# Another engine for one bank copy, and an earlier turn of four feature blocks, in a squared-ReLU MLP on one Trainium2 core

## Chip, core and metric

One Trainium2 chip, one of its cores. The metric is device microseconds of one execution of the whole program; the time of a kernel is the median of its runs. TensorE multiplies out of SBUF into PSUM; ScalarE and VectorE move results out of PSUM and prepare weights; DMAs load the weights.

## The reference

A decoder trunk of two layers on 256 tokens of width 2048, in float32. Each layer has a mixer (recurrent in layer 0, attention in layer 1), a residual add, and an MLP; the change concerns the MLP alone:

```python
def squared_relu_mlp(h, w1, w2):
    return jnp.square(jax.nn.relu(h @ w1)) @ w2
...
        h = h + mix
        h = h + squared_relu_mlp(rms_norm(h, norm_mlp[layer]), mlp_w1[layer], mlp_w2[layer])
```

`w1` is 2048 x 8192 and `w2` 8192 x 2048. Everything must come out with float32 precision.

## The kernel before

**Precision.** Every weight tile `raw` (128 x 2048) is split into `hi`, rounded by ScalarE (L102), and `lo = raw - hi` by VectorE (L103), and each operand likewise; a product is then three matmuls, hi·hi, hi·lo and lo·hi (`times`, 12 matmuls of 512 columns for four feature blocks). Weight tiles are fetched two units ahead, in the order of the list `units`, with three buffers each for `raw`, `hi` and `lo`.

**The MLP.** Each layer's MLP runs over four quarters of 2048 hidden features. In a quarter, `first` makes two pairs (n0 = 0, then n0 = 2) of hidden blocks of 512 with `w1`, and `second` two pairs of output blocks with `w2`. Both go through `blocks`. Half of a pair's work, on feature blocks 0 to 7, is done by seven products in Strassen's manner (`a`, `t1`, `t2`, `c`, `t3`, `d`, `t4`) on sums and differences of weights (`s`, `t`) and of operands (`formx`, `formh`); the other half, on blocks 8 to 15, by plain products (`n2`, `n3` for the one hidden block of the pair, `n6`, `n7` for the other), each for both halves of the tokens. The order for the first matrix is a, t1, n6, t2, c, n7, t3, d, n2, t4, n3. Products are collected in four PSUM banks, alpha, beta, gamma, delta: a and t2 go to beta, t1 and c to alpha. Some products are needed twice. Then an event behind the product copies the bank as it stands into an SBUF tile (`hold`: y1 after a, y4 after t1, y2 after t2), and the bank is added to further. n6 is 12 matmuls into delta and then 12 into alpha, so the alpha half has to wait until t1's content has been copied to y4. In the second matrix the event behind such a product is a VectorE operation that adds the bank into the residual (`to_x`, L751).

**Feature blocks.** The MLP reads its operand with features on partitions. The output projection before it (`out_project`) ends with tokens on partitions; `to_features(n)` turns four feature blocks of it with eight transposes on TensorE, and ScalarE (L235) and VectorE (L236) scale and split them into `bufa`. It is not run at once but put on the list `later`; `flush` runs what is on the list. `tokens` flushes after each weight tile, and `blocks` after each plain product what was on the list when that product began. So `to_features(3)`, blocks 12 to 15, put there at the end of `out_project`, is run behind n6 of the layer's first pair; n7 is the product that reads these blocks. The hidden blocks are turned in the same way for the second matrix (`to_h`), where the tiles of the first pair of hidden blocks (y4 and y2 among them) serve as scratch for the sums in `formh` (L593, L594) while the second pair runs.

**Order.** TensorE's order is the program's: `mm` and `turn` chain every matmul and transpose to the one before. The order on the other engines is set by the tile framework's planner when the kernel is built: at the time it reckons for each point it takes, of the instructions that are ready on an engine, the one with the highest priority. Weight work has its place in the program moved ahead by 150 (`stream`), results of banks and features by 400 (`urgent`). On the chip each engine then runs its list in that order.

Of the kernel before, what the change touches and what calls it, by code (L numbers as in the profile page):

```python
# [41 lines left out]
def trunk_kernel(ctx, tc, x, xtok, cols, tab, masks, pos, fin, w_in, w_gate, w_out, w_qkv, w_o, w1, w2, out):  # L42
# [14 lines left out]
    V, A, T = nc.vector, nc.scalar, nc.tensor  # L57
# [4 lines left out]
    bufa = act.tile([P, KB, 2 * S], F32R, name="bufa")  # L62
# [14 lines left out]
    for step in ORDER.split():  # L77
        src, first, n = where[step[0]]
        units.extend((src, first(int(step[1])) + i) for i in range(n))
# [90 lines left out]
    def unit(src, i):  # L170
        u = at[1]
        assert units[u][0] is src and units[u][1] in (None, i), (u, i)
        at[1] += 1
        if u + 2 >= at[0]:
            fetch()
        return made.pop(u)
# [3 lines left out]
    def mm(*args, **kw):  # L180
        chain[:] = [after(T.matmul(*args, **kw), chain)]  # L181
# [6 lines left out]
    def flush(due=None):  # L188
        todo = later[:due]
        del later[:due]  # L190
        for f in todo:
            f()
# [11 lines left out]
    def lut(out_, in_, func, **kw):  # L204
        i = A.activation(out_, in_, func, **kw)
        if luts["kind"] != tables[func]:
            luts.update(kind=tables[func], before=luts["now"], now=[])
        luts["now"].append(after(i, luts["now"][:1] or luts["before"]))
# [436 lines left out]

    nrm = out_project(w_out, "nmlp0", (2, 3, 0, 1))

    def blocks(src, i0, n0, mov, forms, events, final):
        plain = lambda j, k: (mov[:, k, j * P:j * P + P], mov[:, k, S + j * P:S + j * P + P])
        form = lambda f, k: (forms[:, k, 0, f * P:f * P + P], forms[:, k, 1, f * P:f * P + P])  # L650
        side = {"a": lambda i: plain(0, 2 * i), "d": lambda i: plain(0, 2 * i + 1), "t4": lambda i: plain(1, 2 * i + 1),
                "t1": lambda i: form(3, i), "t2": lambda i: form(0, i), "t3": lambda i: form(1, i),
                "c": lambda i: form(2, i)}
        alpha, delta, gamma = (pmm.tile([P, 512], F32, name="p") for _ in range(3))
        beta = psc.tile([P, 512], F32, name="po" if n0 else "pd", bufs=1)
        bank = {"a": beta, "t1": alpha, "t2": beta, "c": alpha, "t3": beta, "d": gamma, "t4": beta}
        sums = {(0, 0): gamma, (0, 1): beta, (1, 0): alpha, (1, 1): delta}
        opened = []

        def times(bank, w, get):  # L660
            for i in range(4):
                h, l = w.part(i * 512, 512)
                xh, xl = get(i)
                mm(bank, xh, h, start=not any(b is bank for b in opened), stop=False, skip_group_check=True)
                opened.append(bank)
                mm(bank, xh, l, start=False, stop=False, skip_group_check=True)
                mm(bank, xl, h, start=False, stop=i == 3, skip_group_check=True)

        plains = [0, 0]
        for what, u in ORDERS[src is w2]:  # L670
            w = unit(src, None if u is None else i0 + 4 * n0 + u)
            if what != "n":
                times(bank[what], w, side[what])
                if what in events:
                    events[what](bank[what])
                continue
            n, g = divmod(u, 4)
            plains[n] += 1
            due = len(later)
            for j in (1, 0) if n else (0, 1):  # L680
                times(sums[n, j], w, lambda i, j=j, g=g: plain(j, 4 * g + i))
                if plains[n] == 2:
                    final(n, j, sums[n, j])
            flush(due)

    def to_h(n, tiles):
        def work():
            ps = []
            for y in tiles:
                ps.append(psc.tile([P, 4, P], F32, name="pl", bufs=2))  # L690
                for i in range(4):
                    turn(ps[-1][:, i], y[:, i * P:i * P + P])
            with urgent():
                for j, p in enumerate(ps):
                    h = bufb[:, 4 * n:4 * n + 4, j * P:j * P + P]
                    A.copy(h, p)
                    V.tensor_tensor(bufb[:, 4 * n:4 * n + 4, S + j * P:S + j * P + P], p, h.bitcast(F32), OP.subtract)
                if n < 2:
                    z = tiles[1].rearrange("p (k c) -> p k c", k=4)
                    A.copy(z, ps[1])  # L700
                    t = tiles[0].rearrange("p (k c) -> p k c", k=4)
                    (s2, s4), (a21, a22), (a11, a12) = (
                        [v.rearrange("p (m two) c -> p two m c", two=2)[:, e] for e in range(2)] for v in (t, z, ps[0]))
                    combos(a22, s2, a21, s4, a11, a21, a12, a22)
                    for v, at in ((z, slice(1, 4, 2)), (t, slice(0, 4, 2))):
                        part_forms(formh, 2 * n, 2, at, v.rearrange("p (m two) c -> p m two c", two=2))
        later.append(work)

    def first(i0, n0):
        keep, tiles = {}, {}  # L710

        def hold(name, bufs=1):
            def event(bank):
                with urgent():
                    keep[name] = pair.tile([P, 512], F32, name=name, bufs=bufs)
                    A.copy(keep[name], bank)  # L716
            return event

        def relu2(n, j, y, src):
            A.activation(y, src, AF.Relu)  # L720
            A.activation(y, y, AF.Square)  # L721
            tiles[n, j] = y
            if (n, 1 - j) in tiles:
                to_h(n0 + n, (tiles[n, 0], tiles[n, 1]))

        def u3(bank):
            with urgent():
                y = keep["y4"]
                V.tensor_tensor(y, y, bank, OP.subtract)
                V.tensor_tensor(y, keep["delta"], y, OP.add)  # L730
                relu2(1, 1, y, y)

        def final(n, j, bank):
            with urgent():
                if (n, j) == (1, 1):
                    keep["delta"] = bank
                elif (n, j) == (0, 1):
                    y = pair.tile([P, 512], F32, name="y21")
                    relu2(0, 1, y, bank)
                else:  # L740
                    y = keep["y2" if n else "y1"]
                    V.tensor_tensor(y, bank, y, OP.subtract if n else OP.add)
                    relu2(n, j, y, y)

        blocks(w1, i0, n0, bufa, formx, {"a": hold("y1", 2), "t1": hold("y4"), "t2": hold("y2"), "t3": u3}, final)

    def second(i0, n0, nrm, r2, r2n, done, gains):
        def to_x(bank, j, n, r, last):
# [21 lines left out]
    def mlp(layer, nrm, nxt, gname):  # L770
        fing = []

        def gains():
            for n, name in enumerate(("y1", "y1", "y2", "y4")):
                fing.append(pair.tile([P, 512], F32, name=name, bufs=2 if n < 2 else 1))
                nc.gpsimd.dma_start(fing[n], bass.AP(tensor=fin.tensor, offset=fin.offset + 512 * n,
                                                     ap=[[0, P], [1, 512]]))

        r2 = nrm.inv_mean()
        r2n = tmp.tile([P, 2], F32, name="r2n", bufs=2)  # L780
        V.tensor_scalar(r2n, r2, -1.0, None, op0=OP.mult)
        if not gname:
            lut(spare, epsc, AF.Sqrt)
        for q in range(4):
            ends = nxt if q == 3 else None

            def done(n):
                if ends is None:
                    return
                if gname:  # L790
                    to_features(n, gname)
                elif n != LAST:
                    at = slice(n * 512, n * 512 + 512)
                    with urgent():
                        for j in range(2):
                            V.tensor_tensor(xres[:, j, at], xres[:, j, at], fing[n], OP.mult)

            for n in (0, 2):
                first(layer * 64 + q * 16, n)
            for n in (0, 2):  # L800
                second(layer * 64 + q * 16, n, ends, r2, r2n, done, gains if ends and not gname and not n else None)
        return fing

    nx1 = Norm()
    mlp(0, nrm, nx1, "nmix1")
    pairs.close()

# [259 lines left out]
```

## Time and profile before

| | |
|---|---|
| three runs | 2179.17, 2179.26, 2180.12 us, median 2179.26 |
| profiled execution | 2178.8 us; span of the profile 2177.0 us |
| busy in the span | TensorE 99%, VectorE 82%, ScalarE 58%, GpSimd 2% |
| granted TensorE clock | 0.999 |
| HBM read | 460.78 MB, 213 GB/s over the span |
| MLP of layer 0, of layer 1 | from about 426 to 1106 us, from about 1490 us to the end |
| second pair of `first`, layer 0: alpha half of n6 starts at | 479.52, 647.92, 816.32, 984.72 us (168.4 apart) |

PE is TensorE, DVE VectorE, ACT ScalarE, POOL GpSimd, SP SyncE. `p`, `pd` and `po` are PSUM banks: alpha, gamma and delta are `p`, beta is `pd` or `po`. The tiles of `hold` are all called `y` in the trace. A row of the timeline gives start, duration, engine, line, operation, output <- inputs, shapes, how many in a row, and in brackets the idle time before it with what ended it; starts of one row to the next are what tells TensorE's pace, since the ends of matmuls are modelled.

### The profile page before, as it was taken

How to read it: one execution, taken by the hardware profiler on the slowest of the kernel's cores; microseconds unless marked ns; L12 is line 12 of the kernel's file. 1: busy time of each engine (PE TensorE's matmuls, PEld its weight loads, DVE VectorE, ACT ScalarE, POOL GpSimd, SP SyncE). 2: the span in 40 equal slices, each digit the busy share in tenths (PEclk: the TensorE clock that was granted, in tenths of full speed). 3: DMA queues.
4: the chain of work that ended last, by engine and by line, in shares of the span. 5: the costliest groups of instructions: out<-in, count | busy, mean ns of one | idle time of the engine just before them, and what ended most of it. 6: DMA issues, size and time to landing. Idle time of an engine off the chain costs nothing.

```text
span 2177.0 us, 27718 instructions
## 1 busy us (share of the span) xinstructions
PE 2148.7 (99%) x11044; PEld 1834.7 (84%) x11044; DVE 1783.6 (82%) x2078; ACT 1261.1 (58%) x1429; POOL 44.6 (2%) x57
## 2 busy tenths in 40 slices
PE   9999999999999999999999999999999999999997
PEld 8999998878888888888788888888888888888886
DVE  7776787779879889888877778667898898898897
ACT  7444485566466566466554544455655755755664
POOL 0000000000000000000000000000000000000000
PEclk9999999999999999999999999999999999999999
DMA  8444445577777677787655554556768777777873
GB/s 317 155 157 170 149 156 207 189 235 240 228 236 248 226 247 232 232 251 231 201 207 169 179 175 163 185 193 213 232 221 258 237 224 238 251 231 224 260 238 129
DMA packets 65857, 464.68 MB, mean 213 GB/s; under 512 B 7344, under 2 KB 8112, under 8 KB 10304
## 3 DMA queue, kind: packets, MB, share of 16 engines
q1 hardware_dynamic: 58176, 410.89, 53.2%
q0 software_dynamic: 7264, 51.42, 12.8%
q8 instruction: 87, 1.43, 0.3%
q10 hardware_dynamic: 288, 0.61, 0.1%
q14 instruction: 42, 0.34, 0.0%
HBM read 460.78 MB, written 2.10 MB: 213 GB/s over the span
## 4 chain that ended last, share of the span: by engine, by line
PE 89%; ACT 5%; DVE 3%; issue 2%; DMA 1%; SPq 0%; DVEq 0%; ACTq 0%
PE p L181 63%; PE po L181 11%; PE pd L181 10%; ACT hi L102 3%; PE pl L184 2%; DVE lo L103 1%; PE pl L476 1%; DMA raw<-in_w 0%; ACT y L720 0%; ACT formh L593 0%; ACT y L716 0%; ACT y L721 0%; PE pl L864 0%; DMA xall<-in_x 0%; PE po L885 0%
## 5 line engine op out<-in xcount | busy, mean ns | idle before, releaser
L102 ACT CAST hi<-raw 128x1024 fp32r<-128x1024 f32 (+2 forms) x486 | 689.2, 1443 | 571.4 <-PE p L181 403.1
L103 DVE TENSOR_TENSOR lo<-raw,hi 128x1024 fp32r<-128x1024 f32 (+2 forms) x486 | 822.3, 1709 | 237.7 <-ACT hi L102 219.3
L181 PE MATMUL p<-hi,bufb 128*128 128x512 f32 x1408 | 448.5, 390 | 2.2 <-DVE xall L751 2.1
L181 PE MATMUL p<-hi,bufa 128*128 128x512 f32 x1280 | 412.5, 392 | 11.3 <-ACT y L716 7.9
L181 PE MATMUL p<-bufa,hi 128*128 128x256 f32 (+1 forms) x1792 | 364.9, 317 | 0.1
L181 PEld LDWEIGHTS p<-hi,bufb 128*128 128x128 f32 x1408 | 264.3, 188 | 60.0 <-DVE xall L751 5.6
L181 PEld LDWEIGHTS p<-bufa,hi 128*128 128x128 f32 x1792 | 294.5, 190 | 18.9 <-DVE hz L418 0.3
L181 PEld LDWEIGHTS p<-hi,bufa 128*128 128x128 f32 x1280 | 240.4, 188 | 65.5 <-ACT y L716 11.3
L181 PE MATMUL p<-lo,bufb 128*128 128x512 f32 x704 | 274.1, 389 | 1.0 <-DVE lo L103 1.0
L181 PE MATMUL p<-bufa,lo 128*128 128x256 f32 x1152 | 255.5, 287 | 0.0
L181 PE MATMUL p<-lo,bufa 128*128 128x512 f32 x640 | 250.5, 391 | 1.9 <-DVE lo L103 1.9
L103 DVE TENSOR_TENSOR lo<-s,hi 128x2048 fp32r<-128x2048 f32 x96 | 219.5, 2287 | 23.2 <-ACT hi L102 21.3
L102 ACT CAST hi<-s 128x2048 fp32r<-128x2048 f32 x96 | 183.7, 1913 | 48.1 <-PE po L181 21.7
L181 PEld LDWEIGHTS p<-bufa,lo 128*128 128x128 f32 x1152 | 189.3, 191 | 2.7
L181 PEld LDWEIGHTS p<-lo,bufb 128*128 128x128 f32 x704 | 132.2, 188 | 28.3 <-DVE lo L103 1.4
L181 PEld LDWEIGHTS p<-lo,bufa 128*128 128x128 f32 x640 | 120.4, 188 | 27.1 <-DVE lo L103 3.2
L130 DVE TENSOR_TENSOR s<-s,raw 128x2048 f32<-128x2048 f32 x48 | 109.6, 2284 | 1.7 <-DMA raw<-in_w 1.7
L181 PE MATMUL pd<-hi,bufa 128*128 128x512 f32 x256 | 84.8, 392 | 0.0
L181 PE MATMUL po<-hi,bufa 128*128 128x512 f32 x256 | 84.8, 392 | 0.0
L181 PE MATMUL p<-hi,formx 128*128 128x512 f32 x256 | 84.0, 389 | 0.0
L181 PE MATMUL p<-hi,formh 128*128 128x512 f32 x256 | 84.0, 389 | 0.0
L103 DVE TENSOR_TENSOR lo<-t,hi 128x2048 fp32r<-128x2048 f32 x32 | 73.2, 2287 | 12.4 <-ACT hi L102 12.4
(281 smaller groups left out, 2765.7 us busy)
## 6 DMA issues: line engine op xcount, KB each, us to landing
raw<-in_w SPq DMA_DIRECT2D x224, 1024.0 KB, 5.1
raw<-in_w_qkv SPq DMA_DIRECT2D x48, 1024.0 KB, 4.9
raw<-in_w_in SPq DMA_DIRECT2D x46, 1024.0 KB, 4.9
t<-in_w SPq DMA_DIRECT2D x32, 1024.0 KB, 5.4
t<-in_w POOLq DMA_DIRECT2D x32, 1024.0 KB, 8.8
raw<-in_w_out SPq DMA_DIRECT2D x16, 1024.0 KB, 4.9
s<-in_w POOLq DMA_DIRECT2D x16, 1024.0 KB, 8.9
raw<-in_w_o SPq DMA_DIRECT2D x16, 1024.0 KB, 4.9
```

Of the source, the lines that this page charges most:

```text
L102: A.copy(h, w)
L103: V.tensor_tensor(l, w, h.bitcast(F32), OP.subtract)
L130: V.tensor_tensor(held[to], held[x], held[y], OP.add)
L181: chain[:] = [after(T.matmul(*args, **kw), chain)]
L184: chain[:] = [after(T.transpose(out_, in_, ident), chain)]
L476: T.matmul(pl[:, j], kq[:, js], halves(qp[:, js], c, True), start=True, stop=True)
```

## The change

In `first`, y4 is copied out of alpha by VectorE (`V.tensor_copy`) where ScalarE did it (`A.copy`); y1 and y2 stay with ScalarE. And in the first pair of each layer's MLP (quarter 0, n0 = 0) `blocks` flushes the list `later` right behind t1, so `to_features(3)` is run between t1 and n6 where it was run between n6 and t2.

```diff
-    def blocks(src, i0, n0, mov, forms, events, final):
+    def blocks(src, i0, n0, mov, forms, events, final, soon=False):
...
                 if what in events:
                     events[what](bank[what])
+                if what == "t1" and soon:
+                    flush()
                 continue
...
-    def first(i0, n0):
+    def first(i0, n0, soon):
...
-        def hold(name, bufs=1):
+        def hold(name, copy, bufs=1):
             def event(bank):
                 with urgent():
                     keep[name] = pair.tile([P, 512], F32, name=name, bufs=bufs)
-                    A.copy(keep[name], bank)
+                    copy(keep[name], bank)
             return event
...
-        blocks(w1, i0, n0, bufa, formx, {"a": hold("y1", 2), "t1": hold("y4"), "t2": hold("y2"), "t3": u3}, final)
+        blocks(w1, i0, n0, bufa, formx, {"a": hold("y1", A.copy, 2), "t1": hold("y4", V.tensor_copy), "t2": hold("y2", A.copy),
+                                             "t3": u3}, final, soon)
...
-                first(layer * 64 + q * 16, n)
+                first(layer * 64 + q * 16, n, q + n == 0)
```

## The prediction

> **What bounds the kernel now.** I read the page first, for who is busy all the time.
>
> ```profile
> span 2177.0 us, 27718 instructions
> ## 1 busy us (share of the span) xinstructions
> PE 2148.7 (99%) x11044; PEld 1834.7 (84%) x11044; DVE 1783.6 (82%) x2078; ACT 1261.1 (58%) x1429; POOL 44.6 (2%) x57
> ```
>
> TensorE is never long without work, so an edit that adds or removes no matmul can only change the time through TensorE's idle gaps. The second view is therefore the table of waits, for TensorE alone (total us, times, longest).
>
> ```profile
> PE p L181 <- ACT y L716: 7.9, 8, 1.0
> PE p L181 <- DVE lo L103: 2.9, 4, 1.0
> PE p L181 <- DVE bufa L236: 2.7, 2, 1.4
> PE p L181 <- DVE xall L751: 2.1, 2, 1.3
> ```
>
> The first and third rows are what the change touches: L716 is the copy out of a bank in `hold`, L236 the low half of the feature blocks. Eight waits of 1.0 and two of 1.35. Where the eight are I found in TensorE's timeline: always in the second pair of the first matrix (n0 = 2), once a quarter of a layer.
>
> ```profile
> 475.43 0.39 PE L181 MATMUL p<-hi,formx 128*128 128x512 f32 x1
> ...
> 478.14 0.39 PE L181 MATMUL p<-hi,bufa 128*128 128x512 f32 x1
> 479.52 0.50 PE L181 MATMUL p<-hi,bufa 128*128 128x512 f32 x1 [0.99 <-ACT y L716]
> 479.86 0.40 PE L181 MATMUL p<-lo,bufa 128*128 128x512 f32 x1
> 480.09 0.62 PE L181 MATMUL p<-hi,bufa 128*128 128x512 f32 x2
> ```
>
> The second product, t1, ends at 475.43 + 0.39 = 475.82 in the bank alpha. Twelve matmuls of n6 go to delta; the thirteenth goes to alpha and must wait until alpha has been copied to y4. Undisturbed, matmuls start every 0.23 us (479.86 to 480.09), so it was due at 478.37 and came at 479.52: 1.15 lost, and the next one came 0.11 late as well (0.34 instead of 0.23). One such wait costs **1.26 us**, more than the 0.99 of the wait's row. Why the copy is late stands in ScalarE's timeline, and what VectorE does meanwhile in its own.
>
> ```profile
> 474.74 1.93 ACT L102 CAST hi<-s 128x2048 fp32r<-128x2048 f32 x1
> 476.55 1.91 ACT L102 CAST hi<-raw 128x2048 fp32r<-128x2048 f32 x1
> 478.37 0.61 ACT L593 CAST formh<-y 128x512 fp32r<-128x512 f32 x1
> 478.88 0.59 ACT L716 COPY y<-p 128x512 f32<-128x512 f32 x1
> ```
>
> ```profile
> 475.46 0.68 DVE L594 TENSOR_TENSOR formh<-y,formh 128x512 fp32r<-128x512 f32 x1
> 476.70 2.29 DVE L103 TENSOR_TENSOR lo<-s,hi 128x2048 fp32r<-128x2048 f32 x1 [0.56 <-ACT hi L102]
> 478.91 2.29 DVE L103 TENSOR_TENSOR lo<-raw,hi 128x2048 fp32r<-128x2048 f32 x1
> 481.11 0.68 DVE L594 TENSOR_TENSOR formh<-y,formh 128x512 fp32r<-128x512 f32 x1
> ```
>
> ScalarE rounds two weight tiles and one form before it takes the copy, 3.06 after t1's end. VectorE has a hole of 0.56 at exactly that time, in front of `lo<-s`, which waits for ScalarE's `hi<-s` (474.74 + 1.93 = 476.67).
>
> **The change, part by part.**
>
> *The y4 copy in the second pairs (8 times).* It leaves ScalarE and joins VectorE. The trace has no plain VectorE copy of a bank; the nearest is L742, which reads a bank of the same shape and adds another tile:
>
> ```profile
> L742 DVE TENSOR_TENSOR y<-p,y 128x512 f32<-128x512 f32 x4 | 2.8, 688 | 2.4 <-PE p L181 2.4
> ```
>
> I take 0.69 for the copy; the bounds are ScalarE's 0.59 and L751's 0.74 (quoted below). [...]
>
> When can it start? It needs t1's end (475.82) and the tile y4, which in the second pair is still scratch for the preceding `formh` parts: the L594 at 475.46 reads it and ends at 476.14. That is on VectorE itself. At 476.14 the copy is ready and urgent (offset 400), while `lo<-s` is not ready before 476.67 and has a lower rank (150). So it should fill the hole: 476.1 to 476.8, over 1.5 before the matmul is due. The wait goes: **8 × 1.26 = 10.1 us gained**. Behind the copy are queued `lo<-s` and `lo<-raw`; they start some 0.1 later, and for t2 and c, which follow n6's end, that is early enough; the accumulating load on the GpSimd queue that waits for `lo<-s` moves by the same 0.1. ScalarE has less to do.
>
> *The y4 copy in the six ordinary first pairs (n0 = 0, quarters 1 to 3 of each layer).* Today there is no wait. VectorE's and TensorE's rows there:
>
> ```profile
> 602.26 2.29 DVE L103 TENSOR_TENSOR lo<-s,hi 128x2048 fp32r<-128x2048 f32 x1 [0.59 <-ACT hi L102]
> ```
>
> ```profile
> 602.34 0.39 PE L181 MATMUL p<-hi,bufa 128*128 128x512 f32 x1
> ```
>
> n6 starts at 602.34; t1's last result is there 0.16 later, at 602.50 (its last matmul started 0.23 earlier and takes 0.39). `lo<-s` is ready 0.24 before that, so VectorE takes it first, and the copy comes behind it. The second matrix has the same situation today: its t1 event is a VectorE operation of 0.74 (L751), and in its second pair it stands behind `lo<-s`.
>
> ```profile
> 561.13 2.28 DVE L103 TENSOR_TENSOR lo<-s,hi 128x2048 fp32r<-128x2048 f32 x1
> 563.33 0.74 DVE L751 SCALAR_TENSOR_TENSOR xall<-p,nm,xall 128x512 f32<-128x512 f32 x1
> ```
>
> ```profile
> 563.72 0.91 PE L181 MATMUL p<-hi,bufb 128*128 128x512 f32 x2
> 564.47 0.39 PE L181 MATMUL p<-lo,bufb 128*128 128x512 f32 x1
> ```
>
> The split holds the queue for 2.20 (561.13 to 563.33). TensorE loses 0.75 − 2 × 0.23 = 0.29 there. For the first matrix: 602.26 + 2.20 + 0.69 = 605.15, and alpha's half is due twelve starts after 602.34; twelve starts take 478.14 − 475.43 = 2.71, so at 605.05. It is 0.10 late, and with the 0.17 that the second matrix pays beyond its own lateness (the event ends at 564.07, the matmul was due at 563.72 + 0.23 = 563.95; 0.12 of the 0.29) that makes 0.27. **6 × 0.27 = 1.6 lost**; the bounds are 0 (the planner sets the copy ahead of the split) and 6 × 0.29 = 1.7. `lo<-raw` behind it waits for its `hi` anyway.
>
> *The flush behind t1, in the first pair of each layer (twice).* The rows of TensorE and VectorE in layer 0:
>
> ```profile
> 436.82 1.03 PE L184 MATMUL pl<-tab__181,xall 128*128 128x128 f32 x8
> ...
> 444.06 0.39 PE L181 MATMUL p<-lo,bufa 128*128 128x512 f32 x1
> 445.81 0.72 PE L181 MATMUL p<-hi,bufa 128*128 128x512 f32 x2 [1.36 <-DVE bufa L236]
> 446.37 0.40 PE L181 MATMUL p<-lo,bufa 128*128 128x512 f32 x1
> ```
>
> ```profile
> 438.96 2.29 DVE L103 TENSOR_TENSOR lo<-raw,hi 128x2048 fp32r<-128x2048 f32 x1 [2.66 <-ACT hi L102]
> 441.17 0.87 DVE L236 SCALAR_TENSOR_TENSOR bufa<-pl,c__83,bufa 128x256 fp32r<-128x256 f32 x2
> 443.06 2.29 DVE L103 TENSOR_TENSOR lo<-t,hi 128x2048 fp32r<-128x2048 f32 x1 [1.02 <-ACT hi L102]
> 445.27 0.87 DVE L236 SCALAR_TENSOR_TENSOR bufa<-pl,c__83,bufa 128x256 fp32r<-128x256 f32 x2
> ```
>
> n7 needs blocks 12 to 15 and gets the second two 1.75 − 0.23 = 1.52 late, and loses another 0.10 on the restart (0.56 for two): 1.62, in both layers. The eight transposes now come 24 matmuls earlier, 24 × 0.226 = 5.4 us; no DMA goes with them. If the two L236 pairs follow at the same distance, the last is done at 446.14 − 5.4 = 440.7 at the latest, 3.6 before n7 wants it (444.29): a whole split may still slip in. **2 × 1.62 = 3.2 gained**. What it moves: n6's end comes later by the transposes' time, at most 1.03, and with it the buffer for n7's weights, so that their `lo` ends at 441.25 + 1.0 = 442.3; n7's first low matmul is three before the one at 444.06, so at 443.4. That fits by 1.1; if it did not, it would cost up to the 1.62 again. The transposes also stand between t1 and n6 here, so the y4 copy has that much more time and loses nothing.
>
> **Sum:** −10.1 + 1.6 − 3.2 = **−11.7 us**. The profiled execution took 2178.8 us (span 2177.0, 1.8 around it), which gives 2167.1; the median of the three runs, 2179.26, lies 0.5 higher, so **2167.6 us**.
>
> **Rivals.** *The hole is not used (no change).* The planner puts `lo<-s` ahead of the copy in the second pairs as well. The copy then runs from 478.91 to 479.60 and alpha's matmul starts 0.06 later, 479.66 against 479.52 now: 8 × 0.14 = 1.1 worse, and with 1.6 and −3.2 the sum is −0.5: 2178.8. For it: at 561.13 the planner did just that. Against it: there the split was ready first; here it is ready 0.5 after the copy.
>
> *The copy behind both splits (slower).* On ScalarE the planner let two things pass the copy. If on VectorE `lo<-raw` passes too, the copy starts at 481.11, ends at 481.80, and the matmul starts at 481.86: 2.34 later than now, 8 × 2.34 = 18.7, with 1.6 and −3.2 in all +17.1: 2196.4. The whole change turns into a loss when the eight copies end over 0.2 later than today's 479.47. For it: the planner's reckoned times are not the trace's. Against it: by the trace y4 was free at 476.14, before ScalarE chose `hi<-raw`, so the planner reckoned L594 later than it comes; on VectorE the end of L594 is itself the moment of choice, and t1 would have to be reckoned 2.8 us later than it is (478.91 against 476.14).
>
> *VectorE becomes the bound (no change).* The copies add 16 × 0.69 = 11.0 us to it. In the second pair:
>
> ```profile
> 471.00:514.00 43.00, 42.01 (x194) 34.65 (x193) 38.24 (x33) 29.82 (x30) 1.73 (x2) 1.00 0.78 237
> ```
>
> 38.24 of 43.00 are busy (fourth figure); with the copy and without the wait, 38.9 of 41.7, 93%. Were the splits late by each copy, the 11.0 would eat the gain: 2178.6. Against it: the splits wait for ScalarE and so for TensorE, and have holes.
>
> *Half of it.* The features still come late because their splits are ranked behind weights, or some copies miss the hole: 2170 to 2174.
>
> **Chances.** My sum 0.65, half of it 0.07, hole unused 0.09, VectorE bound 0.05, copy behind both splits 0.14. Faster by over 0.2% (4.4 us, about what a measurement here can tell from no change): 0.65 + 0.07 = 0.72. Within: 0.14. Slower: 0.14. The sum's own range is 2164.5 (no loss in the first pairs, which gives 2166.0, and most of the second matrix's 6 × 0.29 gone with other positions in the queues) to 2169; the 8-in-10 range reaches up to the unchanged cases, 2179.
>
> **What would show it.** In the waits of TensorE the rows of L716 and L236 are gone; a new row of a VectorE `y` copy at L716 has six short waits or none. VectorE's timeline has a copy of 0.66 to 0.70 between L594 and `lo<-s` in the second pairs. A quarter without a layer's first pair, 168.4 us now from one such wait to the next (table), is 1.0 shorter. It is wrong if that copy stands behind an L103, or if waits for `lo` grow by as much as L716's shrink.

## The result, and the profile after

The changed kernel takes 2167.25 us (median of 6 runs, 2166.9 to 2167.8) against 2179.22 for the kernel before on the same chips: 12.0 us less, ratio 0.9945 (95% interval 0.9932 to 0.9957). Forecast were 2167.6 and −11.7. The profiled execution took 2166.9 us.

The page of the changed kernel: the span is 11.9 shorter, TensorE's busy time hardly moves, and VectorE carries 16 instructions more.

```profile
span 2165.1 us, 27716 instructions
## 1 busy us (share of the span) xinstructions
PE 2146.9 (99%) x11044; PEld 1833.8 (85%) x11044; DVE 1792.2 (83%) x2094; ACT 1254.1 (58%) x1413; POOL 44.7 (2%) x57
```

So the time came out of gaps. The table of TensorE's waits (total us, times, longest), with line numbers two or three higher than before in this part of the code (L716 is now L718, L751 is L754):

```profile
PE p L181 <- DVE lo L103: 3.3, 4, 1.2
PE p L181 <- DVE xall L754: 2.0, 2, 1.3
```

The rows of L716 (7.9 in 8 waits) and L236 (2.7 in 2) are gone; these two, now the longest, stand as they did, give or take 0.4. For VectorE's copy there is no row of TensorE's matmuls; the six short waits that the prediction allowed for stand with TensorE's weight loads:

```profile
PEld p L181 <- DVE y L718: 2.4, 6, 0.4
```

Laid against the kernel before, matmul for matmul by their starts, each of the eight second pairs is 1.28 shorter, each of the six ordinary first pairs 0.27 to 0.31 longer, and the first pairs of the two layers are 1.67 and 1.65 shorter. That makes −10.24 + 1.67 − 3.32 = −11.89, the whole of the 11.9; what else differs (up to 0.4, in the first 15 us and at a wait for `lo`) cancels out. A quarter is 1.0 shorter, as forecast: the copies of layer 0's second pairs start at 474.33, 641.71, 809.09 and 976.48, 167.4 apart where the waits stood 168.4 apart.

The second pair, where the eight waits were. VectorE's timeline, then TensorE's at the point where alpha's half of n6 begins:

```profile
473.55 0.68 DVE L594 TENSOR_TENSOR formh<-y,formh 128x512 fp32r<-128x512 f32 x1
474.33 0.69 DVE L718 COPY y<-p 128x512 f32<-128x512 f32 x1
474.94 2.28 DVE L103 TENSOR_TENSOR lo<-s,hi 128x2048 fp32r<-128x2048 f32 x1
477.14 2.29 DVE L103 TENSOR_TENSOR lo<-raw,hi 128x2048 fp32r<-128x2048 f32 x1
```

```profile
475.55 0.62 PE L181 MATMUL p<-hi,bufa 128*128 128x512 f32 x2
476.01 0.39 PE L181 MATMUL p<-lo,bufa 128*128 128x512 f32 x1
476.23 0.62 PE L181 MATMUL p<-hi,bufa 128*128 128x512 f32 x2
476.69 0.39 PE L181 MATMUL p<-lo,bufa 128*128 128x512 f32 x1
```

The copy sits in the hole between L594 and `lo<-s` and ends at 475.02. The matmul that needs it is the second of the row at 476.23; the rows go on in steps of 0.23 without a break, 1.4 after the copy.

An ordinary first pair, VectorE and TensorE:

```profile
599.05 2.29 DVE L103 TENSOR_TENSOR lo<-s,hi 128x2048 fp32r<-128x2048 f32 x1 [0.58 <-ACT hi L102]
601.26 0.68 DVE L718 COPY y<-p 128x512 f32<-128x512 f32 x1
601.87 2.28 DVE L103 TENSOR_TENSOR lo<-raw,hi 128x2048 fp32r<-128x2048 f32 x1
```

```profile
601.64 0.86 PE L181 MATMUL p<-hi,bufa 128*128 128x512 f32 x2
602.34 0.40 PE L181 MATMUL p<-lo,bufa 128*128 128x512 f32 x1
```

Here the copy stands behind the split, as in the second matrix, and two starts take 0.70 instead of 0.45: 0.25 lost there in each of the six, and 0.27 to 0.31 with the starts behind them.

A layer's first pair, TensorE and VectorE in layer 0:

```profile
431.14 1.03 PE L184 MATMUL pl<-tab__181,xall 128*128 128x128 f32 x8
...
442.91 0.39 PE L181 MATMUL p<-hi,bufa 128*128 128x512 f32 x1
443.14 0.39 PE L181 MATMUL p<-lo,bufa 128*128 128x512 f32 x1
443.37 0.61 PE L181 MATMUL p<-hi,bufa 128*128 128x512 f32 x2
443.82 0.39 PE L181 MATMUL p<-lo,bufa 128*128 128x512 f32 x1
444.05 0.61 PE L181 MATMUL p<-hi,bufa 128*128 128x512 f32 x2
```

```profile
436.42 0.87 DVE L236 SCALAR_TENSOR_TENSOR bufa<-pl,c__83,bufa 128x256 fp32r<-128x256 f32 x2
437.44 0.88 DVE L236 SCALAR_TENSOR_TENSOR bufa<-pl,c__83,bufa 128x256 fp32r<-128x256 f32 x2 [0.15 <-ACT bufa L235]
439.66 2.29 DVE L103 TENSOR_TENSOR lo<-raw,hi 128x2048 fp32r<-128x2048 f32 x1 [1.34 <-ACT hi L102]
```

The eight transposes run at 431.14, behind t1, and the low halves of the last blocks are written by 438.3; n7 starts at 442.91 and passes 444.05 without the hole of 1.5 that it had there. Its own `lo` is ready at 441.95, 1.2 before its first low matmul at 443.14.

### The profile page after: what moved, and what is told of

It reads as the page before. It is cut to its first block, busy times and chain, and to the rows that moved or that the text cites. A ratio compares the mean times of both kernels' runs of the same rounds, so it can differ in the third digit from the quotient of the medians.

```text
span 2165.1 us, 27716 instructions
## 1 busy us (share of the span) xinstructions
PE 2146.9 (99%) x11044; PEld 1833.8 (85%) x11044; DVE 1792.2 (83%) x2094; ACT 1254.1 (58%) x1413; POOL 44.7 (2%) x57
## 4 chain that ended last, share of the span: by engine, by line
PE 95%; DVE 2%; ACT 1%; DMA 1%; issue 1%; SPq 0%; DVEq 0%; ACTq 0%
PE p L181 67%; PE po L181 12%; PE pd L181 11%; PE pl L184 2%; DVE lo L103 1%; PE pl L476 1%; ACT hi L102 0%; DMA raw<-in_w 0%; PE pl L867 0%; PE po L888 0%; DVE xall L754 0%; DMA xall<-in_x 0%; PE pd L880 0%; PE pd L460 0%; PE pl L866 0%
## 5 line engine op out<-in xcount | busy, mean ns | idle before, releaser
L181 PE MATMUL pd<-hi,bufb 128*128 128x512 f32 x256 | 83.0, 389 | 0.0
```

## Experiments

The theory is that of the prediction: TensorE's gaps are the time. What a copy costs is decided by when it ends against when its bank is due, so by its *place* in its engine's list, and not by which engine carries it or how loaded that engine is. The rivals are that ScalarE's relief helped, that VectorE's load is paid somewhere, and that the two parts of the change need each other. "Before" is each time the kernel before, run on the same chip. The diffs are against the changed kernel, show of each line only what changes, and leave out lines that only keep a name for later use.

**Each part alone.** In `flush_only`, y4 stays with ScalarE:

```diff
-"t1": hold("y4", V.tensor_copy)
+"t1": hold("y4", A.copy)
```

> The early turn alone; y4 stays with ScalarE. Place theory (TensorE's gaps add up, each costs what its starts show): the two waits of n7 for blocks 12 to 15 go, 2 x 1.62 = 3.2, the eight waits for y4 stay: 2179.2 - 3.2 = 2176.0. Rival (the wait only moves, to the weights of n7 or to the transposes' own input): 2179.2, with new TensorE waits for L103 or L236 in the first pair of a layer.

Measured: 2176.14 against 2179.62, −3.5, ratio 0.9985 (0.9976 to 0.9994). In `copy_only` the list is not flushed early:

```diff
-                first(layer * 64 + q * 16, n, q + n == 0)
+                first(layer * 64 + q * 16, n, False)
```

> The VectorE copy of y4 alone; the last feature blocks are turned behind n6 as before. Place theory: 8 x 1.26 gained in the second pairs, 6 x 0.25 lost in the ordinary first pairs (0.25 from the changed kernel's trace), nothing in a layer's first pair, where VectorE takes the copy before the split: 2179.2 - 10.1 + 1.5 = 2170.6. Rival (the two parts need each other, because the copy on VectorE delays the low halves of blocks 12 to 15): those two waits grow by a copy each, 2 x 0.69, 2172.0 or more.

Measured: 2170.89 against 2179.62, −8.7, ratio 0.9960 (0.9947 to 0.9972). TensorE's waits say which part removes which row. The longest row of the kernel with the early turn alone, then of that with the copy alone (neither has the other's):

```profile
PE p L181 <- ACT y L718: 7.9, 8, 1.0
```

```profile
PE p L181 <- DVE bufa L236: 2.7, 2, 1.4
```

The two parts add up, −3.5 − 8.7 = −12.2 against −12.0 together, and the expected 3.2 and 8.6 are met within 0.3. Each interval is 2 to 3 us wide on either side, so the sum alone would not prove it; the rows do, each gone in one kernel and whole in the other: the parts do not need each other.

**Same engine, another place.** `behind_one` orders the y4 copy of the second pairs behind `lo<-s`, still on VectorE:

```diff
-                    copy(keep[name], bank)
+                    after(copy(keep[name], bank), [made[at[1] + 1].rest.name] if name == "y4" and n0 else [])
```

> As changed, but in the second pairs the VectorE copy of y4 is ordered behind the split lo<-s. Nothing else changes place. Place theory (what counts is when the copy ends against when alpha is due): the copy ends 0.14 later than ScalarE's did, the eight waits are back and 0.14 longer: 2167.3 + 8 x (1.26 + 0.14) = 2178.5. Rival (what helped is that ScalarE was relieved of 16 copies, or that VectorE is the better reader): 2167 to 2170.

Measured: 2178.85 against 2179.62, ratio 0.9996 (0.9987 to 1.0005): the gain is gone. What is left, 0.8, is near the 0.7 expected (2179.2 − 2178.5), but not clear of the noise. VectorE's timeline and TensorE's:

```profile
474.95 2.29 DVE L103 TENSOR_TENSOR lo<-s,hi 128x2048 fp32r<-128x2048 f32 x1 [0.55 <-ACT hi L102]
477.16 0.68 DVE L718 COPY y<-p 128x512 f32<-128x512 f32 x1
```

```profile
477.90 0.50 PE L181 MATMUL p<-hi,bufa 128*128 128x512 f32 x1 [1.11 <-DVE y L718]
```

The hole of 0.55 stays empty, and TensorE waits 1.11 where it waited 0.99 for ScalarE. By the starts, each of the eight second pairs is 1.41 longer than in the changed kernel. This is the prediction's rival "the hole is not used", made on purpose.

**Same place, the other engine.** `act_ahead` has the early turn, leaves y4 to ScalarE, and in the second pairs orders the copy ahead of the rounding of c's weights:

```diff
-                    copy(keep[name], bank)
+                    (passed if name == "y4" and n0 else []).append(copy(keep[name], bank).ins.name)
...
+        after(made[u].rounded, [passed.pop()] if what == "c" and passed else [])
```

> Early turn as changed, y4 copied by ScalarE everywhere, but in the second pairs ordered ahead of the rounding of c's weights. Place theory: ScalarE can copy from 476.7 to 477.3 of the earlier trace, ahead of the due 478.4, so the eight waits go without VectorE, and the six short waits of the first pairs do not arise: 2179.2 - 3.2 - 10.1 = 2165.9, 1.5 below the changed kernel. Rival (ScalarE's load): it keeps its 16 copies, 2176.

Measured: 2166.13 against 2179.62, −13.5, ratio 0.9936 (0.9924 to 0.9949). ScalarE's timeline in the second pair:

```profile
473.74 1.92 ACT L102 CAST hi<-s 128x2048 fp32r<-128x2048 f32 x1
475.56 0.62 ACT L593 CAST formh<-y 128x512 fp32r<-128x512 f32 x1
476.07 0.59 ACT L718 COPY y<-p 128x512 f32<-128x512 f32 x1
476.55 1.93 ACT L102 CAST hi<-raw 128x2048 fp32r<-128x2048 f32 x1
```

The copy stands ahead of `hi<-raw` now (L593, which it follows, has come forward with it). All 16 copies are on ScalarE and the waits are gone all the same. With `behind_one` this settles it: the place is the cause, not the engine. Moving the copy to VectorE was one way to get it a better place.

`copy_split` is the changed kernel with ScalarE's copy in the six ordinary first pairs only:

```diff
-"t1": hold("y4", V.tensor_copy)
+"t1": hold("y4", V.tensor_copy if n0 or soon else A.copy)
```

> As changed, but in the six ordinary first pairs ScalarE copies y4 again, where it had no wait. Place theory: the six short waits of 0.25 go: 2167.3 - 1.5 = 2165.8. Rival (noise, or ScalarE's copy delays a rounding that VectorE and TensorE then wait for): 2167.3 or more.

Measured: 2165.90 against 2179.47, −13.6, ratio 0.9937 (0.9924 to 0.9949); the changed kernel had −12.0, so the six short waits were worth 1.6. That is within the two intervals, but the starts say the same: the six places are 0.27 to 0.31 shorter each than in the changed kernel, 1.7 in all, of which a new wait for `bufb` L699 late in layer 1 takes 0.5 back. It and `act_ahead` agree within their spread.

**Load.** `y2_on_v` gives VectorE 16 more copies:

```diff
-"t2": hold("y2", A.copy)
+"t2": hold("y2", V.tensor_copy)
```

> As changed, and y2 is copied by VectorE too: 16 more copies of 0.69, each behind the two L699 operations, 8 us before the bank is due; nothing else changes place. Place theory: no wait arises, 2167.3. Rival (VectorE is the bound, so that what it does more is paid): 16 x 0.69 = 11.0 more, 2178.3.

Measured: 2167.57 against 2179.47, ratio 0.9946 (0.9934 to 0.9959), the changed kernel's time. The second pair of this kernel in the table by stretches (busy us of PE, PEld, DVE, ACT, POOL):

```profile
469.00:511.00 42.00, 42.00 (x195) 34.97 (x194) 39.61 (x35) 29.30 (x28) 1.73 (x2) 1.00 0.78 244
```

VectorE is busy 39.61 of 42.00 and TensorE still all of it. At 94% VectorE is not the bound there.

`y1_on_v` moves y1 and not y2, also 16 copies, but with another list as its result:

```diff
-"a": hold("y1", A.copy, 2)
+"a": hold("y1", V.tensor_copy, 2)
```

> As changed, and y1 is copied by VectorE too: again 16 more copies, but the planner now sets y4 in the second pairs behind both splits and both L594 operations. Place theory: y4 then ends some 4.2 after alpha is due, 4.35 with the restart, in 8 pairs: 2167.3 + 35 = 2202. Rival (load): 2178 as with y2. Rival (the place in the list does not matter, since a copy takes the hole when it comes): 2167.

Measured: 2218.8 (2215.71 to 2219.8) against 2179.47, ratio 1.0178 (1.0164 to 1.0192): 39 us slower than before, and 17 more than the 2202 worked out for the place alone. VectorE's list of the second pair, and TensorE's timeline at its end:

```profile
475.06 2.28 DVE L103 TENSOR_TENSOR lo<-s,hi 128x2048 fp32r<-128x2048 f32 x1
477.26 0.69 DVE L594 TENSOR_TENSOR formh<-y,formh 128x512 fp32r<-128x512 f32 x1
477.86 2.29 DVE L103 TENSOR_TENSOR lo<-raw,hi 128x2048 fp32r<-128x2048 f32 x1
480.06 0.69 DVE L594 TENSOR_TENSOR formh<-y,formh 128x512 fp32r<-128x512 f32 x1
480.66 0.69 DVE L718 COPY y<-p 128x512 f32<-128x512 f32 x1
```

```profile
481.40 0.80 PE L181 MATMUL p<-hi,bufa 128*128 128x512 f32 x1 [3.75 <-DVE y L718]
482.00 0.63 PE L181 MATMUL p<-lo,bufa 128*128 128x512 f32 x1
482.42 1.05 PE L181 MATMUL p<-hi,bufa 128*128 128x512 f32 x2
```

On VectorE L594 comes after `lo<-s`, and y4, which needs L594, comes last of all. ScalarE's list has turned as well: without y1 it takes `hi<-s` ahead of L593, whose result L594 needs; in the changed kernel L593 comes first (472.31) and `hi<-s` second (472.83).

```profile
472.54 1.90 ACT L102 CAST hi<-s 128x2048 fp32r<-128x2048 f32 x1
474.34 0.61 ACT L593 CAST formh<-y 128x512 fp32r<-128x512 f32 x1
```

Whether VectorE's additional copy or ScalarE's missing one turned the order, no run here separates. Behind the wait the matmuls start 0.42 apart (482.00 to 482.42) where they started 0.23 apart, so the clock has dropped too (granted share 0.67 from 481 to 486, in the last section). By the starts, the span is 52.8 longer than the changed kernel's: 32.1 are the eight delays with their restarts, 17.5 the slow starts behind them. What the place theory had not in it is that second price.

`behind_two` is the prediction's slower rival itself: the changed kernel, with y4 behind both splits in the second pairs (the copy is put into the program behind the fetch of c's weights, and made to follow their split).

```diff
+            if soon is None and n0 and u == 6: events["t1"](bank["t1"])
...
+                    after(copy(keep[name], bank), [made[at[1] + 1].rest.name] if name == "y4" and n0 else [])
```

> As changed, but in the second pairs the VectorE copy of y4 is ordered behind both splits, lo<-s and lo<-raw: the prediction's slower rival, made on purpose. Place theory alone: 2.34 later than ScalarE's copy was, so each wait costs 1.26 + 2.34 = 3.60 instead of nothing: 2167.3 + 8 x 3.60 = 2196.1. Rival (a longer idle time of TensorE also costs clock, as in the run with y1 on VectorE, where after 3.75 idle the starts were 0.427 apart instead of 0.227 for some 12 matmuls): up to 8 x 2.4 more, 2215; if 3.3 idle is too short for that, 2196.

Measured: 2211.22 (2208.45 to 2212.95) against 2179.25, ratio 1.0144 (1.0127 to 1.0161): 15 above the place alone. TensorE's waits and its timeline at the first of them:

```profile
PE p L181 <- DVE y L718: 26.5, 8, 3.3
```

```profile
481.76 0.50 PE L181 MATMUL p<-hi,bufa 128*128 128x512 f32 x1 [3.31 <-DVE y L718]
...
483.71 0.63 PE L181 MATMUL p<-lo,bufa 128*128 128x512 f32 x1
484.13 1.05 PE L181 MATMUL p<-hi,bufa 128*128 128x512 f32 x2
484.99 0.63 PE L181 MATMUL p<-lo,bufa 128*128 128x512 f32 x1
```

The place has its price as worked out: each wait holds TensorE up by 3.47 over a normal start, and with the restart's 0.11 that is 3.58 against 3.60. The eleven starts behind it are 0.15 to 2.37 longer than normal, restart included, differently for each of the eight, 11.9 in all (worked out from the eight timelines). The transposes and products behind these take 2.7 more. That is 42.4 with the waits, of the 44.3 by which the profiled span is longer than the changed kernel's; nearly all of the rest lies in the first 25 us of the program, where the two kernels are alike. Behind one of the eight waits, at 1734.21, the starts go on 0.23 apart: there the place has its price and the clock none.

**A version that beats both.** `split_and_event` adds to `copy_split` what `act_ahead` taught, for the second matrix: there the event behind t1 is an addition on VectorE, so in the second pairs `lo<-s` is ordered behind it.

```diff
-"t1": lambda b: to_x(b, 1, n0 + 1, r2, False),
+"t1": lambda b: to_x(b, 1, n0 + 1, r2, False) if not n0 else after(made[at[1] + 1].rest, [to_x(b, 1, n0 + 1, r2, False).ins.name]),
```

> As copy_split, and in the second pairs of the second matrix the VectorE event behind t1 is ordered ahead of the split lo<-s. Place theory: the six waits of 0.29 that stand there (three quarters in each layer) go as well, 1.7: 2165.8 - 1.7 = 2164.1. Rival (the split, now 1.0 later, is late for t2): same as copy_split or slower.

Measured: 2161.12 (2160.44 to 2161.48) against 2179.47, ratio 0.9915 (0.9902 to 0.9929): 4.8 below `copy_split` where 1.7 was expected. VectorE's timeline in a second pair of the second matrix:

```profile
558.22 0.74 DVE L754 SCALAR_TENSOR_TENSOR xall<-po,nm,xall 128x512 f32<-128x512 f32 x1
559.18 0.75 DVE L754 SCALAR_TENSOR_TENSOR xall<-p,nm,xall 128x512 f32<-128x512 f32 x1 [0.21 <-PE p L181]
559.85 2.28 DVE L103 TENSOR_TENSOR lo<-s,hi 128x2048 fp32r<-128x2048 f32 x1
```

VectorE waits 0.21 for t1 and takes the split afterwards. I had counted six places; the last quarter of each layer has the same one, and there the wait was the long one of the table, `xall L754` with 2.0 in two. That row is gone in this kernel's waits. By the starts around them these two were worth 2.6 (in `copy_split` 1.12 and 1.72 from one start to the next in place of 0.23, and 0.11 on each restart), so 1.7 + 2.6 = 4.3; the profiled span is 4.4 shorter (2164.1 to 2159.7). That these agree so closely is partly luck: by the starts the six places give 1.9 and the two 2.7, `copy_split`'s wait for `bufb` L699 is gone, 0.5, and 0.9 is lost in the first 25 us of the program.

## Why the prediction was right

- *The bound.* That only TensorE's gaps count held in every run but the two with waits of over 3 us (3.31 in `behind_two`, 3.71 to 3.75 in `y1_on_v`).
- *The price of a wait, 1.26 and not the row's 0.99.* `behind_one` and `act_ahead` are 12.7 apart. The eight idle times of 1.11 in `behind_one`'s row make 8.9 of that; priced from the starts, 1.40 each, they make 11.2, and with 1.5 for the six short waits the 12.7. Against the kernel before, the second pairs show 1.28 each.
- *The copy's length.* 0.69 taken from L742's row; the 16 copies took 0.68 to 0.69 (681 to 692 ns). No run shows the 0.66 that is the lower end of the forecast's 0.66 to 0.70. That it is longer than ScalarE's 0.59 did not matter, since in the second pairs it ends 1.4 early.
- *The hole.* The planner set the copy between L594 and `lo<-s` in all eight second pairs, as forecast. The prediction's reason, that on VectorE the end of L594 is itself the moment of choice, fits this, but `y1_on_v` shows how little it takes for another order; that the planner chose for this reason is not shown.
- *The ordinary first pairs.* 0.27 each was expected, 0.27 to 0.31 seen from the starts; taking the second matrix's row as the model was right. Together 1.6, measured 1.6 with `copy_split`.
- *The early turn.* 3.2 expected, 3.5 measured, 3.3 by the starts. The low halves came 5.7 before the matmul at 444.05, which is the one that waited, more than the 3.6 allowed, because VectorE took them one behind the other. n7's `lo` had 1.2 to spare; 1.1 was worked out.
- *The layer's first pair.* "Loses nothing" held, though the copy came ahead of the split there, at 431.34, and not behind it.
- *VectorE as the bound* is refuted by `y2_on_v` (39.61 of 42.00 busy, and 2167.57 against the changed kernel's 2167.25).
- *The slower rival was mis-sized.* Its 2196.4 was made of the wait alone. Made on purpose it takes 2211: the mechanism and its 2.34 each were right, the clock behind such waits was missing (granted share 0.83 from 478 to 486 of `behind_two`, with starts up to 0.43 apart). And its condition was nearer than the prediction had it. It named an error of 2.8 us in the planner's reckoning; moving one more copy of 0.69 to VectorE was enough.

## What to carry over

When a short copy stalls the bound engine, look at what stands ahead of it in its engine's list, before moving it to another engine: ordering it ahead of one rounding of weights on the old engine brought at least as much here as moving it (13.5 in `act_ahead`, 12.0 in the changed kernel). Price a wait from the starts of the matmuls around it, not from the idle time of its row, and look for an operation in the same position elsewhere in the trace to price the one that is not there yet. A planner's list is fragile: moving the copy of y1 in place of that of y2 made a difference of 51 us, so read the order of the lists after every such edit.

## What was not expected of the hardware

A TensorE idle time of 1.0 to 1.4 us (0.99 and 1.36 in the kernel before, 1.11 in `behind_one`) cost the later start and 0.10 to 0.11 on the next one; the starts behind it kept their 0.23. Idle times of 3.31 and of 3.71 to 3.75 us were followed by starts 0.43 apart: in `behind_two` behind seven of the eight waits, for five to eleven of the next eleven starts, and behind the eighth for none; in `y1_on_v` behind all eight, for six to eleven. Granted clock in the stretch behind a wait of `y1_on_v`, in the table by stretches (sixth figure after the stretch's length, behind the busy times of PE to POOL):

```profile
481.00:486.00 5.00, 4.60 (x16) 3.71 (x17) 0.35 (x1) 0.17 (x1) 0.00 (x0) 0.67 1.00 257
486.00:500.00 14.00, 14.00 (x66) 11.69 (x65) 11.06 (x12) 10.32 (x11) 0.00 (x0) 1.00 0.68 239
```

0.67 behind the wait, 1.00 afterwards, with starts 0.43 apart against 0.23. What decides how many starts are slow no run here shows: eight equal waits of 3.31 in `behind_two` were followed by delays from 0.15, little more than the restart's 0.11, to 2.37 us. Nor do the runs show from what idle time on it happens: none of the waits in their tables lies between 1.4 and 3.31 us, and of the eight of 3.31 one was followed by no slow start.
